# One 512-column matmul for both parts of x in the first feed-forward projections of a two-block transformer

## The chip, the cores and the metric

The kernel runs on one core of one Trainium2 chip. The metric is device time in microseconds (us), the median of the runs shown. The core has a matrix engine (TensorE, PE; its weight loads are PEld), a vector engine (VectorE, DVE), a scalar engine (ScalarE, ACT), GpSimd (POOL) and DMA queues, here issued almost all by SyncE (SP). They run at the same time and wait for each other by semaphores. Matmul results land in PSUM, eight banks of 128 x 512 fp32 values; everything else is in SBUF, 128 partitions wide.

## What is computed

Two transformer blocks of two layers each, on 256 tokens of width 1024, all in fp32. The parts that the change touches are the feed-forwards; the mixers and attentions around them stay as they are.

```python
def squared_relu_mlp(h, w1, w2):      # 1024 -> 4096 -> 1024, once in each layer of the first block
    a = jax.nn.relu(h @ w1)
    return (a * a) @ w2

def swiglu(x, w_in, w_out):           # 1024 -> 2 x 2816 -> 1024, twice in each layer of the second
    gate, up = jnp.split(x @ w_in, 2, axis=-1)
    return (jax.nn.silu(gate) * up) @ w_out

# first block:  x = x + rmsnorm(squared_relu_mlp(rmsnorm(x, g4), w1, w2), g5)
# second block: h = h + 0.5 * swiglu(rms_norm(h, norm), w_in, w_out)
```

## The kernel before, in words

Activations lie transposed: 128 features of a chunk on the partitions, 256 tokens along the row, eight chunks for the width of 1024. To reach fp32 accuracy every matmul operand is a sum of two fp32r values, a high part (rounded) and a low part (the rest), and every product is three matmuls that accumulate into the same place of a bank: high weight x high x (L216), low weight x high x (L217), high weight x low x (L218), all in `mm3`. The x operands are two tiles, `xhi` and `xlo`, or, for the inner activations, pieces of work tiles that the trace calls `u`.

The weights come in 568 groups of 128 x 1024. `load` fetches one by SP's DMA queue into one of six `raw` tiles; `split` makes `rhi` on ScalarE (L203) and `rlo` = raw - rhi on VectorE (L241), in two halves of 512 columns, into a ring of seven. `take` hands a group to a stage, `done` frees it, and `pump` splits ahead as far as the ring reaches. A scheduler places the instructions of a stage on each engine by their dependences, so an engine's order is not that of the source.

A feed-forward of the second block (`ffn`) has 22 jobs. Job j is `W1(j)`: two groups (gate and up), 8 chunks of x each, so 16 products, 48 matmuls, into the two halves of one bank that `bank()` picks in turn from banks 4 to 7. Then `evac_row` multiplies the bank by the norm's factor per token on VectorE (L209, `u<-ps,rst`), ScalarE takes the Silu, VectorE multiplies by the other half, ScalarE and VectorE make the high and low parts. `W2(j - 2)` follows on TensorE: 24 matmuls that accumulate into banks 0 to 3, which hold the eight output chunks. The last two chunks of `W2` are done by `rows_tail`, bank by bank, so that the closing work of a bank (the residual sum on VectorE, L212 `xres<-ps,xres`) can start while the other banks still accumulate. The MLP of the first block (`mlp`) is alike with 16 jobs of two groups; its first two jobs run together, product by product (`W1(0, 1)`), then the sums of squares for the norm are taken by `rstd_row` (matmuls L447 on a bank from `bank()`), and the evacuation is one VectorE instruction with the relu (L212 `u<-ps,rst`).

The SBUF tiles are allocated one after another in `Kern.__init__`; `xhi` and `xlo` are the columns 12 to 2060 of tiles of 2064, so they begin 48 bytes past the tile's start.

Of the kernel before, what the change touches and what calls it, by code (L numbers as in the profile page):

```python
# [9 lines left out]
F32R = mybir.dt.float32r  # L10
# [91 lines left out]

class Kern:
    def __init__(self, nc, tc, ctx, d):
# [12 lines left out]
        self.rhi = [R(1024, f"rhi{i}") for i in range(RING)]  # L117
        self.rlo = [R(1024, f"rlo{i}") for i in range(RING)]
        self.x = F(2048, "xres")
        self.xh, self.xl = (R(2064, nm)[:, 12:2060] for nm in ("xhi", "xlo"))  # L120
        self.ssum = F(512, "ssum")
        self.sqb = [F(512, f"sqb{i}") for i in range(2)]
        self.nrm = [F(8, f"nrm{i}") for i in range(3)]
# [4 lines left out]
        self.inv = F(64, "inv")  # L128
        self.lbc = F(12, "lbc")
        self.mx = [F(16, f"mx{i}") for i in range(4)]  # L130
# [133 lines left out]
    def proj(self, out, spec, xh=None, xl=None):  # L264
        xh = self.xh if xh is None else xh
        xl = self.xl if xl is None else xl
        wh, wl = self.take(spec)
        for k in range(8):
            self.mm3(out, wh[:, k * 128:(k + 1) * 128], wl[:, k * 128:(k + 1) * 128],
                     xh[:, k * 256:(k + 1) * 256], xl[:, k * 256:(k + 1) * 256], k == 0, k == 7)  # L270
        self.done()

    def projs(self, jobs, xh=None, xl=None):

        xh = self.xh if xh is None else xh
        xl = self.xl if xl is None else xl
        ws = [[self.take(spec) for spec in specs] for _, specs in jobs]
        for k in range(8):
            for (ps, _), w in zip(jobs, ws):
                for o, (wh, wl) in enumerate(w):  # L280
                    self.mm3(ps[:, o * 256:(o + 1) * 256], wh[:, k * 128:(k + 1) * 128], wl[:, k * 128:(k + 1) * 128],
                             xh[:, k * 256:(k + 1) * 256], xl[:, k * 256:(k + 1) * 256],
                             k == 0 and o == 0, k == 7 and o == len(w) - 1, skip=True)
        self.done(sum(len(w) for w in ws))

    def proj_toks(self, jobs, name, xh=None, xl=None):
        xh = self.xh if xh is None else xh
        xl = self.xl if xl is None else xl
        ws = [[self.take((name, "tok", c0, h)) for h in range(2)] for _, c0 in jobs]
        R = lambda z: z.bitcast(F32R)  # L290
        for k in range(8):
            for (ps, _), w in zip(jobs, ws):
                wh, wl = (R(z[:, (k % 4) * 256:(k % 4 + 1) * 256]) for z in w[k // 4])
                for t in range(2):
                    ah = R(xh[:, k * 256 + t * 128:k * 256 + (t + 1) * 128])
                    al = R(xl[:, k * 256 + t * 128:k * 256 + (t + 1) * 128])
# [6 lines left out]
    def proj_tok(self, ps, name, c0, xh=None, xl=None):  # L303
        self.proj_toks([(ps, c0)], name, xh, xl)

    def proj_wide(self, pss, name, c0, xh=None, xl=None):

        xh = self.xh if xh is None else xh
        xl = self.xl if xl is None else xl
        R = lambda z: z.bitcast(F32R)  # L310
        for q in range(4):
            wh, wl = self.take((name, "wide", c0, q))
            for k in (2 * q, 2 * q + 1):
                h, l = (R(z[:, (k % 2) * 512:(k % 2 + 1) * 512]) for z in (wh, wl))
                for t in range(2):
                    ah = R(xh[:, k * 256 + t * 128:k * 256 + (t + 1) * 128])
                    al = R(xl[:, k * 256 + t * 128:k * 256 + (t + 1) * 128])
# [34 lines left out]
    def prep(self, c, gain, x=None, xh=None, xl=None):  # L352
        x = self.x if x is None else x
        xh = self.xh if xh is None else xh
        xl = self.xl if xl is None else xl
        g = self.gc(gain[0], gain[1] * 8 + c)
        X, H, L = (self.chunk(t, c) for t in (x, xh, xl))
# [3 lines left out]
    def prep_hi(self, c, gain):  # L361
        g = self.gc(gain[0], gain[1] * 8 + c)
        self.act(self.chunk(self.xh, c).bitcast(F32R), self.chunk(self.x, c), AF.Identity, scale=g)

    def prep_lo(self, c, gain):
        g = self.gc(gain[0], gain[1] * 8 + c)
        self.stt(self.chunk(self.xl, c).bitcast(F32R), self.chunk(self.x, c), g, self.chunk(self.xh, c),
                        ALU.mult, ALU.subtract)
# [73 lines left out]
    def rstd_row(self):  # L442

        ps = self.bank()
# [24 lines left out]
    def start(self):  # L469
# [27 lines left out]
        self.mh, self.ml = self.big(2, F32R), self.big(2, F32R)  # L497
        self.jobs = []

    def mem_start(self, mem):  # L500
        for b in range(4):
            self.a.dma_start(mem[:, b * 512:(b + 1) * 512], self.d["mem"][:, b * 512:(b + 1) * 512])
        for b in range(4):
            for c in (2 * b, 2 * b + 1):
                self.prep(c, ("mg", 0), mem, self.mh, self.ml)
# [938 lines left out]
```

## Time and profile before

| | |
|---|---|
| median of 3 runs | 1817.27 us (1816.97 to 1817.39) |
| the profiled execution | 1817.29 us, its span 1815.6 us |
| busy, share of the span | PE 97%, PEld 95%, DVE 68%, ACT 57%, POOL 6% |
| DMA | 307.80 MB, mean 170 GB/s |
| matmuls | 14362, of them 12720 from L216 to L218 |

A matmul's own duration in the trace (some 0.28 us for 256 columns) covers its way through the array, and consecutive ones overlap; the distance from one start to the next is what the engine's time is made of. Timeline rows give the start and the duration in us, and an "x2" where the view put two alike in one row. The span is measured on the core; the device time of the same execution is 1.7 us more.

### The profile page before, as it was taken

How to read it: one execution, taken by the hardware profiler on the slowest of the kernel's cores; microseconds unless marked ns; L12 is line 12 of the kernel's file. 1: busy time of each engine (PE TensorE's matmuls, PEld its weight loads, DVE VectorE, ACT ScalarE, POOL GpSimd, SP SyncE). 2: the span in 40 equal slices, each digit the busy share in tenths (PEclk: the TensorE clock that was granted, in tenths of full speed). 3: DMA queues.
4: the chain of work that ended last, by engine and by line, in shares of the span. 5: the costliest groups of instructions: out<-in, count | busy, mean ns of one | idle time of the engine just before them, and what ended most of it. 6: DMA issues, size and time to landing. Idle time of an engine off the chain costs nothing.

```text
span 1815.6 us, 35979 instructions
## 1 busy us (share of the span) xinstructions
PE 1768.7 (97%) x14362; PEld 1722.0 (95%) x14362; DVE 1241.9 (68%) x2261; ACT 1033.0 (57%) x2037; POOL 110.3 (6%) x128
## 2 busy tenths in 40 slices
PE   8899999999999989998999999999999999999997
PEld 7899999999889989998999998999999999899997
DVE  7877786557787685557656778766586566876564
ACT  6556565556566465555544667645465455774453
POOL 2420000000000000000000002000010000200000
PEclk9999999999999999999999999999999999999999
DMA  7434446554654435554555553455545555335551
GB/s 278 158 117 140 160 141 211 187 186 157 223 167 136 158 127 189 188 189 143 187 192 190 174 176 133 170 185 182 196 166 188 188 179 177 121 129 187 196 176 35
DMA packets 85624, 307.80 MB, mean 170 GB/s; under 512 B 9680, under 2 KB 10320, under 8 KB 85456
## 3 DMA queue, kind: packets, MB, share of 16 engines
q1 hardware_dynamic: 83952, 300.92, 48.9%
q0 software_dynamic: 640, 3.15, 0.6%
q8 instruction: 112, 1.84, 0.4%
q10 hardware_dynamic: 864, 1.44, 0.2%
q14 instruction: 56, 0.46, 0.1%
HBM read 304.42 MB, written 1.05 MB: 168 GB/s over the span
## 4 chain that ended last, share of the span: by engine, by line
PE 87%; DVE 6%; ACT 3%; issue 2%; POOL 1%; DMA 1%; DVEq 0%; SPq 0%; ACTq 0%
PE ps L218 25%; PE ps L217 25%; PE ps L216 25%; DVE rlo L241 2%; ACT u L191 1%; PE ps L300 1%; PE ps L299 1%; PE ps L318 1%; PE ps L298 1%; PE ps L320 1%; PE ps L319 1%; PE ps L911 1%; DVE u L212 1%; DVE u L209 1%; PE ps L929 1%
## 5 line engine op out<-in xcount | busy, mean ns | idle before, releaser
L203 ACT CAST rhi<-raw 128x512 fp32r<-128x512 f32 (+1 forms) x1138 | 670.4, 618 | 630.3 <-PE ps L218 591.8
L241 DVE TENSOR_TENSOR rlo<-raw,rhi 128x512 fp32r<-128x512 f32 (+1 forms) x1138 | 760.0, 692 | 336.0 <-ACT rhi L203 331.0
L216 PE MATMUL ps<-xhi,rhi 128*128 128x256 f32 x2560 | 721.8, 282 | 16.1 <-ACT xhi L191 9.5
L218 PE MATMUL ps<-xlo,rhi 128*128 128x256 f32 x2560 | 724.1, 283 | 4.8 <-DVE xlo L212 4.8
L217 PE MATMUL ps<-xhi,rlo 128*128 128x256 f32 x2560 | 724.5, 283 | 0.0
L216 PEld LDWEIGHTS ps<-xhi,rhi 128*128 128x128 f32 x2560 | 488.5, 191 | 18.8 <-ACT xhi L191 10.7
L218 PEld LDWEIGHTS ps<-xlo,rhi 128*128 128x128 f32 x2560 | 484.7, 189 | 7.0 <-DVE xlo L212 6.7
L217 PEld LDWEIGHTS ps<-xhi,rlo 128*128 128x128 f32 x2560 | 485.1, 190 | 0.7 <-DVE rlo L241 0.3
L216 PE MATMUL ps<-u,rhi 128*128 128x256 f32 x1680 | 474.3, 282 | 0.0
L217 PE MATMUL ps<-u,rlo 128*128 128x256 f32 x1680 | 471.0, 280 | 0.0
L218 PE MATMUL ps<-u,rhi 128*128 128x256 f32 x1680 | 471.0, 280 | 0.0
L216 PEld LDWEIGHTS ps<-u,rhi 128*128 128x128 f32 x1680 | 317.5, 189 | 0.9 <-issue 0.7
L218 PEld LDWEIGHTS ps<-u,rhi 128*128 128x128 f32 x1680 | 317.3, 189 | 0.7 <-DVE u L206 0.6
L217 PEld LDWEIGHTS ps<-u,rlo 128*128 128x128 f32 x1680 | 317.3, 189 | 0.4 <-issue 0.2
L209 DVE TENSOR_TENSOR u<-ps,rst 128x512 f32<-128x512 f32 (+1 forms) x129 | 84.0, 655 | 105.2 <-PE ps L218 104.8
L209 POOL TENSOR_TENSOR ssum<-ssum,sqb 128x512 f32<-128x512 f32 x26 | 38.0, 1463 | 1268.8 <-ACT sqb L191 1267.2
L191 ACT ACTIVATE u<-u 128x256 f32<-128x256 f32 (+3 forms) x158 | 86.3, 549 | 35.3 <-PE ps L701 17.5
L206 DVE TENSOR_TENSOR u<-u,u 128x256 fp32r<-128x256 f32 (+2 forms) x128 | 66.4, 519 | 10.3 <-ACT u L203 10.1
L203 ACT CAST u<-u 128x256 fp32r<-128x256 f32 (+2 forms) x128 | 61.9, 483 | 11.5 <-POOL u L1176 7.5
L212 DVE SCALAR_TENSOR_TENSOR xlo<-xres,gain,xhi 128x256 fp32r<-128x256 f32 x96 | 56.9, 620 | 3.0 <-ACT xhi L191 3.0
L191 ACT ACTIVATE xhi<-xres,gain 128x256 fp32r<-128x256 f32 x96 | 43.4, 500 | 26.2 <-DVE xres L209 19.7
L209 DVE TENSOR_TENSOR u<-u,u 128x256 f32<-128x256 f32 (+2 forms) x107 | 51.1, 479 | 0.6 <-ACT u L191 0.5
(170 smaller groups left out, 1260.0 us busy)
## 6 DMA issues: line engine op xcount, KB each, us to landing
raw<-w SPq DMA_DIRECT2D x567, 512.0 KB, 3.9
u<-bias POOLq DMA_DIRECT2D x8, 384.0 KB, 3.9
xres<-x SPq DMA_DIRECT2D x4, 256.0 KB, 5.4
u<-mem ACTq DMA_DIRECT2D x4, 256.0 KB, 3.6
raw<-w SPq DMA_DIRECT2D x2, 256.0 KB, 4.4
u<-tabs SPq DMA_DIRECT2D x1, 512.0 KB, 4.2
out<-u SPq DMA_DIRECT2D x2, 256.0 KB, 2.7
u<-masks SPq DMA_DIRECT2D x1, 256.0 KB, 6.9
```

Source lines behind the costliest of these rows:

```text
L191: i = self.a.activation(out, in_, func, scale=scale, **kw)
L203: return self.a.copy(out.bitcast(F32R), in_)
L206: return self.v.tensor_tensor(out.bitcast(F32R), in_, hi, ALU.subtract)
L209: return (eng or self.v).tensor_tensor(out, a, b, op)
L212: return self.v.scalar_tensor_tensor(out, a, s, b, op0, op1)
L216: self.pe.matmul(out, R(wh), R(xh), start=start, stop=False, skip_group_check=skip)
L217: self.pe.matmul(out, R(wl), R(xh), start=False, stop=False, skip_group_check=skip)
L218: self.pe.matmul(out, R(wh), R(xl), start=False, stop=stop, skip_group_check=skip)
L241: b = self.v.tensor_tensor(l[:, c].bitcast(F32R), r[:, c], h[:, c], ALU.subtract)
L298: self.pe.matmul(o, ah, wh, start=k == 0 and t == 0, stop=False, skip_group_check=True)
L299: self.pe.matmul(o, ah, wl, start=False, stop=False, skip_group_check=True)
L300: self.pe.matmul(o, al, wh, start=False, stop=k == 7 and t == 1, skip_group_check=True)
```

## The change

`xhi` and `xlo` become one tile `xpair` in which every chunk's high part (256 columns) is followed by its low part (`Pair`). A new `projs2` is used for the first projections of `mlp` and `ffn` alone. For each product it issues one matmul of 512 columns, high weight x (high, low), over a whole bank, and one of 256 columns, low weight x high x, into the second half. The sum of the two halves of a bank is then the result. So a job of two groups now has two banks (`pair_bank`: 4 and 5, or 6 and 7), and `halves` adds the halves of each by a VectorE reduction into the SBUF tile that the old evacuation now reads and writes. `rstd_row` of these stages uses bank 3. All other products still go through `mm3`, with views of `xpair`. The order of the small tiles is changed so that `xpair` begins at a multiple of 512 bytes and `rlo` 480 bytes past one.

The core of the diff; the other hunks replace the pair of arguments `xh, xl` by `xp` everywhere.

```diff
@@ class Kern, __init__ @@
         self.rhi = [R(1024, f"rhi{i}") for i in range(RING)]
+        self.inv = F(64, "inv")
+        self.mx = [F(16, f"mx{i}") for i in range(3)]
+        self.nrm = [F(8, "nrm0")]
         self.rlo = [R(1024, f"rlo{i}") for i in range(RING)]
+        self.nrm.append(F(8, "nrm1"))
         self.x = F(2048, "xres")
-        self.xh, self.xl = (R(2064, nm)[:, 12:2060] for nm in ("xhi", "xlo"))
+        self.xp = Pair(R(4096, "xpair"))
...
+    def pair_bank(self):
+        self.nbank += 3 - self.nbank % 2
+        i = 4 + self.nbank % 4
+        return self.psum[i - 1], self.psum[i]
+
+    def projs2(self, jobs):
+
+
+        ws = [[self.take(spec) for spec in specs] for _, specs in jobs]
+        R = lambda z: z.bitcast(F32R)
+        for k in range(8):
+            c = slice(k * 128, (k + 1) * 128)
+            for (ps, _), w in zip(jobs, ws):
+                for o, (wh, wl) in enumerate(w):
+                    self.pe.matmul(ps[o], R(wh[:, c]), R(self.xp.both(k)),
+                                   start=k == 0, stop=False, skip_group_check=True)
+                    self.pe.matmul(ps[o][:, 256:512], R(wl[:, c]), R(self.xp.h(k)),
+                                   start=False, stop=k == 7, skip_group_check=True)
+        self.done(sum(len(w) for w in ws))
+
+    def halves(self, out, pair):
+
+        for o, ps in enumerate(pair):
+            self.v.tensor_reduce(self.chunk(out, o), ps.rearrange("p (s b) -> p b s", s=2), AX.X, ALU.add)
...
-    def rstd_row(self):
-
-        ps = self.bank()
+    def rstd_row(self, ps=None):
+
+        ps = self.bank() if ps is None else ps
...
@@ mlp @@
-            pss = [self.bank() for _ in js]
-            self.projs([(p, [("w_ff1", "col", l, (2 * j + o) * 128) for o in range(2)]) for p, j in zip(pss, js)])
+            pss = [self.pair_bank() for _ in js]
+            self.projs2([(p, [("w_ff1", "col", l, (2 * j + o) * 128) for o in range(2)]) for p, j in zip(pss, js)])
             if "r" not in st:
-                st["r"] = self.rstd_row()
+                st["r"] = self.rstd_row(self.psum[3])
             for ps, j in zip(pss, js):
                 t, a, ah, al = B[j % m]
-                self.stt(self.two(t), self.two(ps), 0.0, self.row(st["r"], 2), ALU.max, ALU.mult)
+                self.halves(t, ps)
+                self.stt(self.two(t), self.two(t), 0.0, self.row(st["r"], 2), ALU.max, ALU.mult)
...
@@ ffn @@
-            pss = [self.bank() for _ in js]
+            pss = [self.pair_bank() for _ in js]
             jobs = [(p, [(wi, "col", l, o + j * 128) for o in (0, DFF)]) for p, j in zip(pss, js)]
             for j in jobs:
-                self.projs([j])
+                self.projs2([j])
...
-                self.evac_row(t, ps, st["r"])
+                self.halves(t, ps)
+                self.evac_row(t, t, st["r"])
```

TensorE in the third of the four feed-forwards of the second block, at the end of its last first projection (job 21) and the beginning of a second projection, before. `u116` holds the inner activation of job 19, the number behind an underscore is a tile's running number:

```order
L216 MATMUL ps6_117<-xhi_89,rhi5_79 128x256
L217 MATMUL ps6_117<-xhi_89,rlo5_86 128x256
L218 MATMUL ps6_117<-xlo_90,rhi5_79 128x256
L216 MATMUL ps6_117<-xhi_89,rhi6_80 128x256
L217 MATMUL ps6_117<-xhi_89,rlo6_87 128x256
L218 MATMUL ps6_117<-xlo_90,rhi6_80 128x256
L216 MATMUL ps0_111<-u116_14200,rhi0_74 128x256
L217 MATMUL ps0_111<-u116_14200,rlo0_81 128x256
L218 MATMUL ps0_111<-u116_14200,rhi0_74 128x256
```

The same place in the change; the lines of the file have moved, L251 to L253 are now `mm3`:

```order
L332 MATMUL ps6_116<-xpair_95,rhi5_79 128x512
L334 MATMUL ps6_116<-xpair_95,rlo5_91 128x256
L332 MATMUL ps7_117<-xpair_95,rhi6_80 128x512
L334 MATMUL ps7_117<-xpair_95,rlo6_92 128x256
L251 MATMUL ps0_110<-u116_13135,rhi0_74 128x256
L252 MATMUL ps0_110<-u116_13135,rlo0_86 128x256
L253 MATMUL ps0_110<-u116_13135,rhi0_74 128x256
```

Three matmuls of 256 columns have become one of 512 and one of 256, and the two groups of the job write two banks.

VectorE at the same place: the evacuation of job 21, the product with the gate, the low part (`u115` as output) and the first closing sum, before:

```order
L241 TENSOR_TENSOR rlo6_87<-raw3_71,rhi6_80 128x512
L209 TENSOR_TENSOR u112_14196<-ps6_117,rst2_103 128x512
L241 TENSOR_TENSOR rlo5_86<-raw2_70,rhi5_79 128x512
L209 TENSOR_TENSOR u114_14198<-u114_14198,u112_14196 128x256
L241 TENSOR_TENSOR rlo6_87<-raw3_71,rhi6_80 128x512
L206 TENSOR_TENSOR u115_14199<-u114_14198,u115_14199 128x256
L241 TENSOR_TENSOR rlo0_81<-raw4_72,rhi0_74 128x512 x2
L212 SCALAR_TENSOR_TENSOR xres_88<-ps0_111,xres_88 128x512
```

And in the change, where L341 is `halves`, L276 the split of the weights, L244 the evacuation and the gate product, L241 the low part, L247 the closing sum:

```order
L276 TENSOR_TENSOR rlo6_92<-raw3_71,rhi6_80 128x512
L341 TENSOR_REDUCE u112_13131<-ps6_116 128x256
L341 TENSOR_REDUCE u112_13131<-ps7_117 128x256
L276 TENSOR_TENSOR rlo5_91<-raw2_70,rhi5_79 128x512
L244 TENSOR_TENSOR u112_13131<-u112_13131,rst2_106 128x512
L276 TENSOR_TENSOR rlo6_92<-raw3_71,rhi6_80 128x512
L244 TENSOR_TENSOR u114_13133<-u114_13133,u112_13131 128x256
L276 TENSOR_TENSOR rlo0_86<-raw4_72,rhi0_74 128x512
L241 TENSOR_TENSOR u115_13134<-u114_13133,u115_13134 128x256
L276 TENSOR_TENSOR rlo0_86<-raw4_72,rhi0_74 128x512
L247 SCALAR_TENSOR_TENSOR xres_94<-ps0_110,xres_94 128x512
```

Two reductions and one more split stand between the end of the first projection and the evacuation.

TensorE at the end of the same feed-forward (`rows_tail`; rhi0 and rlo0 are weights of chunk 19, rhi1 of chunk 20, rhi2 of chunk 21), before:

```order
L216 MATMUL ps3_114<-u116_14200,rhi0_74 128x256
L217 MATMUL ps3_114<-u116_14200,rlo0_81 128x256
L218 MATMUL ps3_114<-u116_14200,rhi0_74 128x256
L216 MATMUL ps0_111<-u115_14199,rhi1_75 128x256
L217 MATMUL ps0_111<-u115_14199,rlo1_82 128x256
L218 MATMUL ps0_111<-u115_14199,rhi1_75 128x256
L216 MATMUL ps0_111<-u115_14199,rhi2_76 128x256
L217 MATMUL ps0_111<-u115_14199,rlo2_83 128x256
L218 MATMUL ps0_111<-u115_14199,rhi2_76 128x256
L216 MATMUL ps0_111<-u115_14199,rhi1_75 128x256
L217 MATMUL ps0_111<-u115_14199,rlo1_82 128x256
```

In the change, from the third of the four banks on:

```order
L251 MATMUL ps2_112<-u115_13134,rhi1_75 128x256
L252 MATMUL ps2_112<-u115_13134,rlo1_87 128x256
L253 MATMUL ps2_112<-u115_13134,rhi1_75 128x256
L251 MATMUL ps3_113<-u115_13134,rhi1_75 128x256
L252 MATMUL ps3_113<-u115_13134,rlo1_87 128x256
L253 MATMUL ps3_113<-u115_13134,rhi1_75 128x256
L251 MATMUL ps0_110<-u115_13134,rhi2_76 128x256
L252 MATMUL ps0_110<-u115_13134,rlo2_88 128x256
L251 MATMUL ps1_111<-u115_13134,rhi2_76 128x256
```

Before, the first product of chunk 21 (rhi2) followed one product of chunk 20 (rhi1); now it follows four, one for each of the banks 0 to 3, so nine matmuls of chunk 20 have moved ahead of it.

## Rows read from the trace of the kernel before

**Rows 1.** The profile's page: busy, granted clock, and the chain that ended last.

```profile
span 1815.6 us, 35979 instructions
...
PE 1768.7 (97%) x14362; PEld 1722.0 (95%) x14362; DVE 1241.9 (68%) x2261; ACT 1033.0 (57%) x2037; POOL 110.3 (6%) x128
...
PEclk9999999999999999999999999999999999999999
...
PE 87%; DVE 6%; ACT 3%; issue 2%; POOL 1%; DMA 1%; DVEq 0%; SPq 0%; ACTq 0%
PE ps L218 25%; PE ps L217 25%; PE ps L216 25%; DVE rlo L241 2%; ACT u L191 1%; PE ps L300 1%; PE ps L299 1%; PE ps L318 1%; PE ps L298 1%; PE ps L320 1%; PE ps L319 1%; PE ps L911 1%; DVE u L212 1%; DVE u L209 1%; PE ps L929 1%
```

**Rows 2.** Timeline of TensorE, 1511 to 1520 us (start, duration, engine, line, operation).

```profile
1511.36 0.28 PE L216 MATMUL ps<-u,rhi 128*128 128x256 f32 x1
...
1514.16 0.28 PE L216 MATMUL ps<-xhi,rhi 128*128 128x256 f32 x1
...
1519.83 0.28 PE L216 MATMUL ps<-u,rhi 128*128 128x256 f32 x1
```

**Rows 3.** Timeline of TensorE where it has 512 columns.

```profile
453.05 0.39 PE L318 MATMUL ps<-rhi,xhi 128*128 128x512 f32 x1
...
458.60 0.39 PE L318 MATMUL ps<-rhi,xhi 128*128 128x512 f32 x1
...
1130.12 0.62 PE L1223 MATMUL ps<-u,exact 128*128 128x512 f32 x2
1130.57 0.40 PE L1225 MATMUL ps<-u,exact 128*128 128x256 f32 x2
```

**Rows 4.** Groups of VectorE by form: count | busy, mean ns | idle before.

```profile
L209 DVE TENSOR_TENSOR u<-ps,rst 128x512 f32<-128x512 f32 x113 | 77.5, 690 | 105.0 <-PE ps L218 104.8
...
L403 DVE TENSOR_SCALAR nrmw<-ps 128x256 f32<-128x256 f32 x16 | 6.7, 416 | 2.2 <-ACT nrmw L191 2.2
...
L870 DVE TENSOR_REDUCE mx<-ps 128x2 f32<-128x512 f32 x8 | 5.5, 689 | 3.5 <-PE ps L911 3.5
```

**Rows 5.** Busy us (and instructions) of PE, PEld, DVE, ACT, POOL by stretch; clock.

```profile
240.00:434.00 194.00, 193.91 (x1646) 193.50 (x1645) 126.88 (x208) 108.29 (x191) 2.84 (x2) 1.00 0.54 185
...
1352.00:1534.00 182.00, 182.00 (x1548) 181.84 (x1547) 114.09 (x199) 91.26 (x174) 2.34 (x3) 1.00 0.55 188
```

**Rows 6.** Timelines at the third feed-forward's end: DVE, then PE.

```profile
1528.49 0.69 DVE L209 TENSOR_TENSOR u<-ps,rst 128x512 f32<-128x512 f32 x1 [1.19 <-PE ps L218]
1529.10 0.68 DVE L241 TENSOR_TENSOR rlo<-raw,rhi 128x512 fp32r<-128x512 f32 x1
1529.70 0.42 DVE L209 TENSOR_TENSOR u<-u,u 128x256 f32<-128x256 f32 x1
...
1531.39 0.42 DVE L206 TENSOR_TENSOR u<-u,u 128x256 fp32r<-128x256 f32 x1 [0.67 <-ACT u L203]
...
1528.29 0.28 PE L216 MATMUL ps<-u,rhi 128*128 128x256 f32 x1
...
1531.44 0.35 PE L216 MATMUL ps<-u,rhi 128*128 128x256 f32 x1
```

**Rows 7.** Timelines at the start of the first MLP: PE, then DVE.

```profile
253.83 0.28 PE L216 MATMUL ps<-xhi,rhi 128*128 128x256 f32 x1
...
265.02 0.28 PE L218 MATMUL ps<-xlo,rhi 128*128 128x256 f32 x1
...
265.38 0.47 PE L216 MATMUL ps<-xhi,rhi 128*128 128x256 f32 x1
...
256.52 0.68 DVE L209 TENSOR_TENSOR u<-ps,mrst 128x512 f32<-128x512 f32 x1
...
261.25 0.68 DVE L209 TENSOR_TENSOR u<-ps,mrst 128x512 f32<-128x512 f32 x1
```

**Rows 8.** Waits of TensorE for x: in all, times, longest; then one in its timeline.

```profile
PE ps L218 <- DVE xlo L212: 4.8, 8, 1.6
...
1541.46 0.39 PE L218 MATMUL ps<-xlo,rhi 128*128 128x256 f32 x1 [0.77 <-DVE xlo L212]
```

## What I expected before the run

> **What bounds the kernel now.** I read the busy shares first, then the chain that ended last: TensorE is busy for 97% of the span, and 87% of the chain is TensorE work, of which the three matmul lines of the shared product helper (L216, L217, L218) carry 25% each [rows 1]. VectorE is busy for 68%. The granted TensorE clock is at its upper level, 2.4 GHz, in all 40 slices [rows 1]. So the time is the number of matmuls times the distance from one start to the next, plus the few places where TensorE waits. The "mean ns of one" of a matmul group is no price, because matmuls overlap; I price by start to start. The waits of TensorE on the feed-forward operands are short: 4.8 us in 8 waits of L218 for the low part of x [rows 8].
>
> The distances, from the timeline of TensorE. In the third of the four feed-forwards a first projection runs from 1514.16 to 1519.83, 48 matmuls of 256 columns in 5.67 us: 118.1 ns each, 354.4 ns for the three passes of a product. The 24 matmuls of the second projection before it, of the same shape, take from 1511.36 to 1514.16: 2.80 us, 116.7 ns each [rows 2]. So a matmul of 256 columns costs 116.7 to 118.1 ns, and what differs between the two is only where their operands lie. For 512 columns the kernel has its own example: from 453.05 to 458.60 run 24 of them, 5.55 us, 231.3 ns each; two others, from 1130.12 to 1130.57, take 225 ns each [rows 3].
>
> The Trainium skill, page "TensorE: Matmul & The Clock Gate", section "Back-to-back issue gap", gives the gap of a single matmul at the full clock as its columns over 2.4 plus about 2.5 ns, which makes an estimated 109.2 and 215.8 ns here. The trace does not agree: its distances are 7% longer, so they decide; the rule comes back beside a rival, since by it the fused matmul saves only one fixed 2.5 ns.
>
> **The change part by part.** *Fused matmuls.* The first projections of both MLPs (2 x 32 column groups) and of the four feed-forwards (4 x 44) are 240 groups of 8 products, 1920 products. Each falls from three matmuls of 256 columns to one of 512 and one of 256, so 5760 matmuls become 3840. A pair costs between 225 + 116.7 = 341.7 and 231.3 + 118.1 = 349.4 ns. I take 346 (229 + 117): 229 since the 24 in a row weigh more than the two, less something because the new buffer for x starts at a multiple of 512 bytes and the low weights are put 480 bytes past one, an arrangement nearer to that of the 116.7 ns matmuls than the old one. Saving: 354.4 - 346 = 8.4 ns x 1920 = **16.1 us**; ends 5.0 ns (9.6 us) and 12.7 ns (24.4 us). No row shows a 512-column matmul with these operands, so no saving at all stays an outer end (last rival).
>
> *Other matmuls whose addresses change.* 640 products with x in other stages and 1680 with an activation move, the first perhaps to the better distance, the others perhaps away from it. Between 116.7 and 118.1 the difference is 1.4 ns a matmul; over 1920 matmuls that is 2.7 us one way, over 5040 it is 7 us the other way. I take **0**.
>
> *The sums on VectorE.* Every one of the 120 jobs (pairs of groups) now has two reductions of one bank, 128x512 to 128x256, ahead of its old evacuation, which then reads SBUF. The nearest row is the 689 ns reduction L870 that reads 128x512 from a bank, though to 128x2; the plain evacuations of 128x512 take 690 [rows 4]. I take 0.69 us; bounds 0.42 (an operation over 128x256, the size written, from a bank) and twice 0.69. That is 2 x 0.69 x 120 = 166 us of VectorE work. It costs TensorE nothing where it is covered: in the third feed-forward 22 jobs fill 182 us with 114.1 us of VectorE work [rows 5], 5.2 us in a period of 8.3 us, and become 6.6; in the first MLP 126.9 us over 16 jobs, 7.9 in a period of 12.1, become 9.3. The cover goes if the reduction takes over (8.3 - 5.2) / 2 = 1.5 us.
>
> *End of each feed-forward.* The last job's result is needed at once. Now: evacuation at 1528.49, a split, the gate product at 1529.70, the low part at 1531.39; TensorE ends the first projection at 1528.29, covers with 24 matmuls of the second projection, and reaches the last operand at 1531.44 [rows 6]. In the change two reductions and one split stand ahead of the evacuation: 3 x 0.60 (VectorE's starts in a row, 1528.49 to 1529.10) = 1.8 us later. The new order puts nine more matmuls of the operand before last ahead, 9 x 0.117 = 1.05 us. What is left is a stall of 0.8 us, plus bank 0 finishing later than the stage's closing work wants it; I take **1.0 us x 4 = 4 us** (0 to 2 each).
>
> *Start of each MLP.* The first two jobs run together and now fill all four rotating banks, where two were used. The third job starts 0.36 us after the last matmul of the second, 265.02 to 265.38 [rows 7]. Its banks are free only after two reductions of the first job, which start when TensorE ends: 2 x 0.60 + about 0.15 of handover less 0.36 = **1.0 us x 2 = 2 us** (1 to 3). In the first MLP the evacuations of memory jobs at 256.52 and 261.25 still hold two of the banks when the second job wants to start at 253.8 [rows 7]; the order moves its matmuls behind the first job's 16 pairs (5.5 us), which covers most. I take **1.3 us** (0 to 2.5).
>
> *First matmul of a stage.* It needs the low part of x as well, two matmuls (0.23 us) earlier than now, in six stages: **1.2 us** (0 to 3; the longest such wait now is 1.6 us, the one shown 0.77 [rows 8]). The norm's row sums go to bank 3, which nobody uses then: 0.
>
> Sum of costs 8.5 us (2 to 15). Net -16.1 + 8.5 = -7.6. The profiled execution is 1817.29 us, the median 1817.27, so **1809.7 us, say 1810**. Ends: -24.4 + 3 gives 1796; -9.6 + 15 gives 1823.
>
> **Rivals.** *Reduction slow, slower than before.* The reduction reads its bank with a step of 256 elements between the two values that it adds, and no row of before shows such a read. The Trainium skill, page "Advanced Engine Details and Errata", section "PSUM Cachelines", states that every two consecutive elements should be contiguous for best throughput; that speaks against this read, and no run here shows it yet. What would happen: each 0.1 us more per reduction costs 0.2 us at each of four ends and two starts, 1.2 us in all. From 1.5 us VectorE bounds the 88 feed-forward jobs too. At 1.7 us: 12 us from the ends and starts, and (5.2 + 3.4 - 8.3) x 88 = 26 us: 1810 + 38 = **1848**. It ends above before from about 1.3 us per reduction on (7.3 / 12 x 0.1 = 0.6 above 0.69). For it: the step. Against: the product and the reduction over 512 elements of a bank both take 0.69, whatever is done with them [rows 4]. Chance 0.11.
>
> *Fusing saves only a fixed part.* The cost per column stays and only the fixed part of one matmul goes: 2 x 116.7 - 231.3 = 2.1 ns x 1920 = 4 us, against 8.5 us of costs: **1822**; with 5.0 ns it is 1816. For it: the 24 in a row at 231.3. Against: 225 at the other place. Chance 0.22, spread over 1815 to 1823. By the formula of the Trainium skill, page and section as above, the saving would be an estimated 2.5 ns a product, 4.8 us, and the time 1821.
>
> *Addresses do more.* If the new arrangement brings the pair to 342 ns and the other 6960 matmuls (2320 products) gain 1 ns each, the gain is 24 + 7 us against 8.5: **1795**. For it: 116.7 against 118.1 in rows of one shape. Against: only 1.4 ns is seen. Chance 0.12.
>
> *The change does not do what it says.* If a 512-column matmul of these operands ran as two of 256, the distance would be 233 or more and the gain under 3 us: 1823. The order shows one instruction, and the 512-column rows are under two of 256. Chance 0.03.
>
> **How the numbers follow.** Main case 0.52, centred on 1810, its own range 1801 to 1817. About 0.2%, 3.6 us, is what a measurement of this kernel can tell from no change: faster is below 1813.6, slower above 1820.9. Faster: 0.44 of the main case, all 0.12 of the addresses, 0.04 of the fixed part: 0.60. Same: 0.08, 0.11 and 0.02 of the slow reduction: 0.21. Slower: 0.19, from the slow reduction 0.09, the fixed part 0.07, the last 0.03. A range of **1795 to 1823** leaves out most of the slow reduction and little below: 2 in 10.
>
> **What would show it.** Right: W1 stretches of the feed-forward with 32 matmuls in about 5.53 us, 0.13 us less than 5.67; reductions at about 0.69 us; VectorE busy near 1410 us of the span; waits of TensorE for VectorE of about 1 us at each feed-forward end and after the second MLP job. Wrong: a pair above 352 ns (fusing pays nothing), a reduction above 1.3 us, waits for the reductions in the middle of the feed-forwards, or distances of the other matmuls that move by over 1 ns.

## The result, and the profile after

The change makes the kernel slower: 1833.11 us median of 5 runs (1831.7 to 1835.26) against 1817.39 (1816.97 to 1818.32), a ratio of 1.0084 with a 95% interval of 1.0071 to 1.0098. The forecast was 1810, faster. All medians here and below are of executions that agree; one of f3_bank_by_bank, 6189.27 us, is left out. The profiled execution of the change is 1833.55 us, its span 1831.8, 16.2 us more than before.

The page of the change, first the busy shares and the clock, then the groups of the new operations (count | busy us, mean ns of one | idle before):

```profile
span 1831.8 us, 32363 instructions
...
PE 1775.8 (97%) x12442; PEld 1638.9 (89%) x12442; DVE 1377.1 (75%) x2501; ACT 1040.0 (57%) x2037; POOL 108.7 (6%) x128
...
PEclk9999999999999999999999999999999999999999
...
L332 PE MATMUL ps<-xpair,rhi 128*128 128x512 f32 x1920 | 690.5, 399 | 13.9 <-DVE xpair L247 12.7
L334 PE MATMUL ps<-xpair,rlo 128*128 128x256 f32 x1920 | 542.4, 283 | 0.0
...
L341 DVE TENSOR_REDUCE u<-ps 128x256 f32<-128x512 f32 x240 | 155.2, 686 | 102.4 <-PE ps L334 102.1
```

The change does what it says: TensorE has 1920 matmuls fewer, at nearly the same mean granted clock (0.988 of full speed against 0.991), and still the same 97% of a longer span [rows 1]. The reductions take 686 ns, as taken (0.69). VectorE's busy time rises by 135 us, less than the 166 forecast in part because neighbours in a row overlap (two reductions take 1.29 us below, not twice 0.69). The chain that ended last is followed back through 14% of this span only, so it is not used; the starts of TensorE are.

Timeline of TensorE in the third feed-forward of the change (start, duration, engine, line, operation): the beginning of a second projection, of a first projection, and of the next second projection.

```profile
1500.74 0.28 PE L251 MATMUL ps<-u,rhi 128*128 128x256 f32 x1
...
1503.57 0.40 PE L332 MATMUL ps<-xpair,rhi 128*128 128x512 f32 x1
...
1509.23 0.28 PE L251 MATMUL ps<-u,rhi 128*128 128x256 f32 x1
```

The first projection now has 32 matmuls and takes 5.66 us, where 48 took 5.67 [rows 2]: 353.8 ns for a pair. The second projection, which the change does not touch, takes 2.83 us for its 24 matmuls, where it took 2.80: 117.9 instead of 116.7 ns each.

For all further comparisons I use means of start to start over a whole trace, of matmuls that follow each other directly, with those more than 25 ns above the median (waits) left out, and add up the two or three of a product. Before, a product with x takes 353.8 ns and one with an inner activation 350.4. In the change the pair takes 353.6 (233.1 + 120.5) and the inner product 353.6. So 1920 products gain 0.4 us in all, and 1680 lose 5.4 us.

The rest is waits. TensorE's waits in the change (us in all, times, longest), those that are new or longer than in [rows 8]:

```profile
PE ps L332 <- DVE xpair L247: 12.7, 4, 5.7
...
PE ps L253 <- DVE xpair L247: 4.1, 4, 2.1
PE ps L251 <- ACT u L238: 4.1, 5, 1.8
...
PE ps L332 <- DVE u L244: 1.2, 1, 1.2
...
PE ps L253 <- DVE u L247: 0.8, 1, 0.8
```

The end of the third feed-forward in the change, VectorE and then TensorE:

```profile
1543.02 1.29 DVE L341 TENSOR_REDUCE u<-ps 128x256 f32<-128x512 f32 x2 [0.95 <-PE ps L334]
1544.22 0.68 DVE L276 TENSOR_TENSOR rlo<-raw,rhi 128x512 fp32r<-128x512 f32 x1
1544.82 0.69 DVE L244 TENSOR_TENSOR u<-u,rst 128x512 f32<-128x512 f32 x1
...
1546.03 0.42 DVE L244 TENSOR_TENSOR u<-u,u 128x256 f32<-128x256 f32 x1
...
1547.71 0.42 DVE L241 TENSOR_TENSOR u<-u,u 128x256 fp32r<-128x256 f32 x1 [0.66 <-ACT u L238]
...
1547.30 0.28 PE L253 MATMUL ps<-u,rhi 128*128 128x256 f32 x1
1547.73 0.39 PE L251 MATMUL ps<-u,rhi 128*128 128x256 f32 x1 [0.15 <-ACT u L238]
1547.95 0.28 PE L252 MATMUL ps<-u,rlo 128*128 128x256 f32 x1
```

From the first reduction to the evacuation pass 1.80 us, the three steps that the prediction counted. TensorE's gap before the last operand is 0.43 us where 0.12 is usual.

The start of the first MLP, TensorE's first matmul of a second projection before:

```profile
276.90 0.28 PE L216 MATMUL ps<-u,rhi 128*128 128x256 f32 x1
```

And in the change, from the first matmul of the stage on; behind it, in the form of [rows 5], a stretch with its clock:

```profile
255.84 0.40 PE L332 MATMUL ps<-xpair,rhi 128*128 128x512 f32 x1
...
276.57 0.39 PE L251 MATMUL ps<-u,rhi 128*128 128x256 f32 x1 [1.79 <-ACT u L238]
...
277.27 0.63 PE L332 MATMUL ps<-xpair,rhi 128*128 128x512 f32 x1
...
277.91 0.63 PE L332 MATMUL ps<-xpair,rhi 128*128 128x512 f32 x1
...
284.08 0.28 PE L253 MATMUL ps<-u,rhi 128*128 128x256 f32 x1
```

```profile
277.20:280.60 3.40, 3.40 (x12) 2.91 (x11) 1.85 (x4) 1.15 (x2) 0.00 (x0) 0.50 0.67 213
```

Before, the first four jobs take from 253.83 [rows 7] to 276.90, 23.07 us. In the change they end at 284.08, 28.24 us after the first matmul. The new order puts two matmuls of the second projection (276.57) ahead of the fourth job, and TensorE waits 1.79 us there for the inner activation; the second MLP has the same wait, 1.80 us at 683.34. Shortly after the first of these waits the granted clock is 0.50, the lower level of 1.2 GHz, for 3.4 us: a pair then takes 0.64 us (277.27 to 277.91) instead of 0.35.

### The profile page after: what moved, and what is told of

Same layout as the page of the kernel before. It is cut to its first block, busy times and chain, and to the rows that moved or that the text cites. A ratio compares the mean times of both kernels' runs of the same rounds, so it can differ in the third digit from the quotient of the medians.

```text
span 1831.8 us, 32363 instructions
## 1 busy us (share of the span) xinstructions
PE 1775.8 (97%) x12442; PEld 1638.9 (89%) x12442; DVE 1377.1 (75%) x2501; ACT 1040.0 (57%) x2037; POOL 108.7 (6%) x128
## 5 line engine op out<-in xcount | busy, mean ns | idle before, releaser
L276 DVE TENSOR_TENSOR rlo<-raw,rhi 128x512 fp32r<-128x512 f32 (+1 forms) x1138 | 762.2, 694 | 247.5 <-ACT rhi L238 237.2
L332 PE MATMUL ps<-xpair,rhi 128*128 128x512 f32 x1920 | 690.5, 399 | 13.9 <-DVE xpair L247 12.7
L334 PE MATMUL ps<-xpair,rlo 128*128 128x256 f32 x1920 | 542.4, 283 | 0.0
L251 PE MATMUL ps<-u,rhi 128*128 128x256 f32 x1680 | 475.3, 283 | 4.1 <-ACT u L238 4.1
L253 PE MATMUL ps<-u,rhi 128*128 128x256 f32 x1680 | 472.5, 282 | 0.8 <-DVE u L247 0.8
L332 PEld LDWEIGHTS ps<-xpair,rhi 128*128 128x128 f32 x1920 | 363.5, 190 | 99.9 <-DVE xpair L247 14.9
L334 PEld LDWEIGHTS ps<-xpair,rlo 128*128 128x128 f32 x1920 | 362.8, 189 | 0.8
L251 PEld LDWEIGHTS ps<-u,rhi 128*128 128x128 f32 x1680 | 316.9, 189 | 11.5 <-ACT u L238 5.6
L253 PEld LDWEIGHTS ps<-u,rhi 128*128 128x128 f32 x1680 | 316.2, 188 | 1.2 <-DVE u L247 1.0
L341 DVE TENSOR_REDUCE u<-ps 128x256 f32<-128x512 f32 x240 | 155.2, 686 | 102.4 <-PE ps L334 102.1
L251 PE MATMUL ps<-xpair,rhi 128*128 128x256 f32 x640 | 186.2, 292 | 7.0 <-ACT rhi L238 7.0
L253 PE MATMUL ps<-xpair,rhi 128*128 128x256 f32 x640 | 182.1, 285 | 4.1 <-DVE xpair L247 4.1
L252 PE MATMUL ps<-xpair,rlo 128*128 128x256 f32 x640 | 182.2, 285 | 0.0
L251 PEld LDWEIGHTS ps<-xpair,rhi 128*128 128x128 f32 x640 | 122.8, 192 | 8.4 <-ACT rhi L238 7.0
L253 PEld LDWEIGHTS ps<-xpair,rhi 128*128 128x128 f32 x640 | 122.7, 192 | 5.2 <-DVE xpair L247 5.0
L252 PEld LDWEIGHTS ps<-xpair,rlo 128*128 128x128 f32 x640 | 124.4, 194 | 0.7 <-DVE rlo L276 0.3
L244 POOL TENSOR_TENSOR ssum<-ssum,sqb 128x512 f32<-128x512 f32 x26 | 37.6, 1447 | 1285.7 <-ACT sqb L226 1285.5
L241 DVE TENSOR_TENSOR u<-u,u 128x256 fp32r<-128x256 f32 (+2 forms) x128 | 66.5, 520 | 6.3 <-ACT u L238 6.1
```

Source lines behind the costliest of these rows:

```text
L241: return self.v.tensor_tensor(out.bitcast(F32R), in_, hi, ALU.subtract)
L244: return (eng or self.v).tensor_tensor(out, a, b, op)
L251: self.pe.matmul(out, R(wh), R(xh), start=start, stop=False, skip_group_check=skip)
L252: self.pe.matmul(out, R(wl), R(xh), start=False, stop=False, skip_group_check=skip)
L253: self.pe.matmul(out, R(wh), R(xl), start=False, stop=stop, skip_group_check=skip)
L276: b = self.v.tensor_tensor(l[:, c].bitcast(F32R), r[:, c], h[:, c], ALU.subtract)
```

## The experiments

Three theories were on trial. **Columns**: a matmul's distance is its columns, so one of 512 costs what two of 256 do, and nothing can be saved. **Places**: fusing does save, but where the operands lie in SBUF moves every distance, and the new places eat the saving. **VectorE**: its extra reads and writes slow TensorE down. All times are medians; ratios are to the kernel before, run on the same chip.

| kernel | us | ratio (95%) | product with x in a first projection, ns | inner product, ns |
|---|---|---|---|---|
| before | 1817.39 | 1 | 353.8 | 350.4 |
| the change | 1833.11 | 1.0084 (1.0071 to 1.0098) | 353.6 | 353.6 |
| e1_old_places | 1824.28 | 1.0033 (1.002 to 1.0046) | 350.0 | 351.6 |
| e2_new_places_alone | 1824.99 | 1.0042 (1.0027 to 1.0057) | 353.2 | 356.2 |
| e3_two_of_256 | 1834.2 | 1.0089 (1.0074 to 1.0104) | 353.9 | 353.9 |
| e4_no_sums | 1823.45 | 1.0033 (1.0022 to 1.0043) | 353.6 | 353.7 |
| f1_fused_at_32 | 1813.73 | 0.9981 (0.9971 to 0.9991) | 346.8 | 350.1 |
| f2_before_at_32 | 1811.11 | 0.9963 (0.9948 to 0.9977) | 350.7 | 350.6 |
| f3_bank_by_bank | 1830.70 | 1.007 (1.0053 to 1.0087) | 353.5 | 353.7 |
| g1_before_at_16 | 1810.86 | 0.996 (0.9945 to 0.9975) | 350.7 | 350.2 |
| g2_more_at_16 | 1820.46 | 1.0009 (0.999 to 1.0027) | 352.6 | 352.2 |
| g3_fused_at_64 | 1824.74 | 1.0028 (1.0018 to 1.0037) | 349.1 | 352.9 |
| h1_old_form_at_ends | 1807.71 | 0.9941 (0.9925 to 0.9958) | 346.7 | 350.3 |
| h2_at_32_two_of_256 | 1822.22 | 1.0022 (1.0012 to 1.0031) | 351.1 | 351.1 |

(In the kernels with three matmuls everywhere, the column for x holds all 2560 products with x.)

### Old places, new places, two for one, no sums

The change with the places of before:

```diff
-        self.inv = F(64, "inv")
-        self.mx = [F(16, f"mx{i}") for i in range(3)]
-        self.nrm = [F(8, "nrm0")]
         self.rlo = [R(1024, f"rlo{i}") for i in range(RING)]
...
-        self.xp = Pair(R(4096, "xpair"))
+        self.xp = Pair(R(4128, "xpair")[:, 12:4108])
```

> The change with the operand places of before: the low weights at a multiple of 512 bytes again, the tile for x 48 bytes past one; everything else as in the change. Columns theory (a matmul's distance is its columns, so one of 512 costs what two of 256 do, wherever the operands lie): the pair stays at 350 to 354 ns, the products with an activation fall back from 353.8 to 350.3 ns, 1680 x 3.5 = 6 us, so about 1827 us. Places theory (fusing would save, the new places eat it): the pair falls to 346 to 348 as well, 1920 x 7 = 13 us more, so about 1814. VectorE theory (its extra reads and writes slow TensorE's operand reads): nothing changes, 1833.

1824.28 us, 0.5% under the change: the pair at 350.0 ns (232.4 + 117.6) and the inner product at 351.6. 1920 x 3.6 + 1680 x 2.0 = 10 us; the times differ by 9. (The low part of x is not quite where it was: 112 bytes past a multiple of 512 before, 48 here.) It fits the columns theory best, which had let the pair fall to 350; VectorE's theory, with nothing to change, falls.

The places of the change alone, with the old matmuls:

```diff
-            pss = [self.pair_bank() for _ in js]
-            self.projs2([(p, [("w_ff1", "col", l, (2 * j + o) * 128) for o in range(2)]) for p, j in zip(pss, js)])
+            pss = [self.bank() for _ in js]
+            self.projs([(p, [("w_ff1", "col", l, (2 * j + o) * 128) for o in range(2)]) for p, j in zip(pss, js)])
...
-                self.halves(t, ps)
-                self.evac_row(t, t, st["r"])
+                self.evac_row(t, ps, st["r"])
```

> The places of the change alone: x in one tile of alternating parts, low weights 480 bytes past a multiple of 512, but three matmuls of 256 columns, one bank for a job and no sums, as before. Columns theory: the products with an activation are at 353 to 354 instead of 350.3 ns, first projections about 353, so 1817 + 6 = 1823 us. Places theory: the first projections too become slower by what the fused matmul lost, 7 ns x 1920 = 13 us, so about 1836. VectorE theory: places do nothing, 1817.

1824.99 us. Moving operands costs 7 us without any change to the work: the inner product goes from 350.4 to 356.2 ns (9.7 us), the products with x from 353.8 to 353.2 (1.5 us back). The inner products lie here as they do in the change, where they take 353.6: so place alone does not settle the distance.

The 512-column matmul written as two:

```diff
-                    self.pe.matmul(ps[o], R(wh[:, c]), R(self.xp.both(k)),
-                                   start=k == 0, stop=False, skip_group_check=True)
+                    self.pe.matmul(ps[o][:, 0:256], R(wh[:, c]), R(self.xp.h(k)),
+                                   start=k == 0, stop=False, skip_group_check=True)
+                    self.pe.matmul(ps[o][:, 256:512], R(wh[:, c]), R(self.xp.l(k)),
+                                   start=False, stop=False, skip_group_check=True)
```

> The change with its 512-column matmul written as two of 256 columns (high weight x high x, high weight x low x), same banks, places and sums. Columns theory: 2 x 117.5 for 235, no change in time, 1833 plus or minus 3 us. Forecast's theory (fusing saves 8 ns a product, the loss is elsewhere): 1833 + 16 = 1849. Places theory: as columns theory, within 3 us.

1834.2 us and 353.9 ns for a product, as the change. At these places fusing saves 0.3 ns a product. Up to here the columns theory had the better of it.

The reductions left out:

```diff
-                self.halves(t, ps)
-                self.evac_row(t, t, st["r"])
+                self.evac_row(t, ps[1], st["r"])
```

> The change without the two reductions of a job: the evacuation reads the second bank of the pair as it is, so the sums of the halves and the first bank's results are left out of the computation. VectorE has the work of before. Columns theory: the products stay at 353.8 ns and the pair at 353 to 355; only the waits at the ends and starts go, 8 to 9 us, so about 1825. VectorE theory: pair and products fall to 348 and 350 as well, 10 + 6 us more, so about 1809.

1823.45 us: the sums cost 9 to 10 us, and the distances stay at 353.6 and 353.7 ns. So VectorE's 155 us of reductions do not lengthen the distances; they cost waits, and perhaps clock. Of the waits shown above, those for ACT's `u` and the 0.8 us for VectorE's `u` are gone; the 1.2 us for VectorE's `u` (L244) stay at 1.1, so they are not the sums'. The mean granted clock over the runs is 0.9915 here and 0.989 in the change. An estimate of the most that this can be worth is (0.9915 - 0.989) x 1830 = 4.6 us, so up to half of the 9 to 10 us may have gone by way of the clock.

### Better places, and a scan of them

Since the inner activations lie 32 bytes past a multiple of 512 and their products took 350 ns, x was put there, first in the change; the diff is to e1:

```diff
-        self.xp = Pair(R(4128, "xpair")[:, 12:4108])
+        self.xp = Pair(R(4128, "xpair")[:, 8:4104])
```

> The change with the low weights at a multiple of 512 bytes and x 32 bytes past one, which is where the inner activations lie whose products take 349.9 ns. Places theory: the pair falls from 350.0 ns (x at 48) to 347 or 348, so 1824 - 5 = 1819 us. If 32 has no merit of its own: 350 ns, 1824.

1813.73 us, 19 us under the change with the same instructions. The pair takes 346.8 ns (228.5 + 118.3), within 1 ns of the price that the prediction had taken; the inner product is back at 350.1. Timeline of TensorE in this kernel, the same three starts as above:

```profile
1508.82 0.28 PE L248 MATMUL ps<-u,rhi 128*128 128x256 f32 x1
...
1511.62 0.39 PE L329 MATMUL ps<-xpair,rhi 128*128 128x512 f32 x1
...
1517.17 0.28 PE L248 MATMUL ps<-u,rhi 128*128 128x256 f32 x1
```

5.55 us for the 32 matmuls instead of 5.66, and 2.80 for the second projection instead of 2.83. Then the same in the kernel before:

```diff
-        self.xh, self.xl = (R(2064, nm)[:, 12:2060] for nm in ("xhi", "xlo"))
+        self.xh, self.xl = R(2056, "xhi")[:, 8:2056], R(2072, "xlo")[:, 0:2048]
```

> The kernel before with both parts of x 32 bytes past a multiple of 512 instead of 48 and 112; nothing else. Places theory: the 2560 products with x go from 353.8 to about 350 ns, 9.7 us, so about 1808 us. If 32 has no merit of its own: 1818.

1811.11 us, 7 us under before by moving two tiles: 350.7 instead of 353.8 ns for 2560 products is 7.9 us. So at the same good places the change (f1, ratio 0.9981) is no faster than the three matmuls (f2, 0.9963): the 3.9 ns a product, 7.5 us, do not pay for the sums.

The two groups of a job one after the other:

```diff
-        for k in range(8):
-            c = slice(k * 128, (k + 1) * 128)
-            for (ps, _), w in zip(jobs, ws):
-                for o, (wh, wl) in enumerate(w):
+        for (ps, _), w in zip(jobs, ws):
+            for o, (wh, wl) in enumerate(w):
+                for k in range(8):
+                    c = slice(k * 128, (k + 1) * 128)
```

> The change with a job's two groups one after the other (8 chunks into one bank, then 8 into the other) instead of alternating product by product. If going to another bank after each pair costs TensorE time, the 256-column matmul falls from 120.5 to about 117.5 ns, 1920 x 3 = 6 us; the first bank's sum can also be taken 2.8 us earlier, which takes 0.6 us off each of the six waits at ends and starts: 1834 - 6 - 4 = 1824. If the bank does not matter: 1834 - 4 = 1830. Columns theory says nothing of banks: 1830.

1830.70 us: 120.4 ns for the 256-column matmul, 120.5 in the change. Going to another bank costs nothing. The wait for ACT's `u` falls from 4.1 to 2.6 us, as earlier sums would have it; the rest of the 2.4 us is not located.

TensorE alone, other engines idle, 32 products in either form at each place (`MOFF` are the offsets of x from a multiple of 512 bytes, `LOFF` those of the low weights):

```diff
+        for a in MOFF:
+            for b in LOFF:
+                three(a, b, 2)
+                two(a, b, 2)
```

> TensorE alone, nothing of the transformer computed: jobs of 16 products as three matmuls of 256 columns and as a pair of 512 and 256, one after the other, for ten places of x and four of the low weights, other engines idle. Columns theory: the pair is shorter than the three by at most 4 ns at every place, 1 to 2 ns in the mean, and both move with the places by several ns. Forecast's theory: the pair is shorter by about 8 ns, at least at the places of the change. VectorE theory: with the other engines idle the distances no longer depend on the places.

Its timeline gives four starts in a row: three matmuls with x at 0 and the low weights at 480 (the places of the change), the pair there, three matmuls with x at 16 and the low weights at 0, and the pair there. Then the same with x at 32 and the low weights at 0, three and pair.

```profile
113.55 0.28 PE L1378 MATMUL ps<-x,wh 128*128 128x256 f32 x1
...
124.85 0.39 PE L1389 MATMUL ps<-x,wh 128*128 128x512 f32 x1
...
136.16 0.28 PE L1378 MATMUL ps<-x,wh 128*128 128x256 f32 x1
...
147.04 0.39 PE L1389 MATMUL ps<-x,wh 128*128 128x512 f32 x1
...
225.80 0.28 PE L1378 MATMUL ps<-x,wh 128*128 128x256 f32 x1
...
236.99 0.40 PE L1389 MATMUL ps<-x,wh 128*128 128x512 f32 x1
...
248.10 0.28 PE L1378 MATMUL ps<-x,wh 128*128 128x256 f32 x1
```

Divided by 32: at the places of the change 353.1 for three and 353.4 for the pair, as in the kernel; with x at 32, 349.7 and 347.2, as in f2 and f1. So the distances are TensorE's own, and VectorE's theory is out. The columns theory in its strict form is out too: over 39 places the pair is 4.6 ns shorter in the mean, and the difference runs from -12 to +24 ns. With x at 16 three matmuls took 340.0, the least seen.

That made 16 look like a gain of 35 us:

```diff
+        x2 = R(4128, "xboth")
+        self.xh, self.xl = x2[:, 4:2052], x2[:, 2052:4100]
```

> The kernel before, three matmuls a product, with both parts of x 16 bytes past a multiple of 512 (in one tile, one after the other). In the scan a product took 340.0 ns there, against 355.0 with x at 48. Places theory: 2560 products x (353.8 - 340.0) = 35 us less, 1783 us. If the scan holds only where the other engines are idle: within 5 us of 1811, what x at 32 gave. Columns theory without places: 1818.

1810.86 us and 350.7 ns: a miss. In the kernel the 340 of the scan does not come. With the inner activations at 16 as well:

```diff
+    def ring16(self, n, width):
+        per = 1000 // width
+        u = [self.unit(F32R) for _ in range(-(-n // per))]
+        return [u[i // per][:, 124 + (i % per) * width:124 + (i % per + 1) * width] for i in range(n)]
```

> The same, and the high and low parts of the inner activations of MLPs and feed-forwards 16 bytes past a multiple of 512 as well, instead of 32. Places theory: 1216 second-projection products from 349.9 towards 340 ns, 12 us less than x at 16 alone: 1771. The order of the weights is another there than in the scan (one x chunk against eight weights), so it may give nothing: then 1783.

1820.46 us, a miss too, and its ten runs spread from 1808.17 to 1826.31, where those of before stay within 4 us. The profiled one has 352.6 and 352.2 ns. In the change, x and the low weights at 64:

```diff
-        self.inv = F(64, "inv")
-        self.mx = [F(16, f"mx{i}") for i in range(3)]
-        self.nrm = [F(8, "nrm0")]
+        self.mx = [F(16, "mx0")]
         self.rlo = [R(1024, f"rlo{i}") for i in range(RING)]
```

> The change with x and the low weights both 64 bytes past a multiple of 512. In the scan a pair took 340.3 ns there, against 353.2 at the places of the change. Places theory: 1920 x (353.6 - 340.3) = 25 us less than the change, 1808 us, the other products as in the change. Columns theory without places: 1834. If the forecast's 8 ns were to come on top: not under 1795.

1824.74 us, between: the pair at 349.1, not the 340.3 of the scan.

> TensorE alone again, nothing of the transformer computed: the three matmuls, the pair, and products in the order of the second projections, for 13 other places of x (steps of 4 bytes up to 28, then 40, 80, 112, 144, 272, 496) and low weights at 0 and 64. If 17/16 of the columns at 2.4 GHz is a floor for both forms (768 columns, 340 ns), no place gives less than 340 to either; if fusing has a saving of its own, some place gives a pair clearly under 340. Products in the order of the second projections: about 350 at no place under 340.

The second scan shows that a place alone does not decide. Three starts with x at 16 and low weights at 0: three matmuls, the pair, and products in the order of the second projections.

```profile
251.12 0.28 PE L1378 MATMUL ps<-x,wh 128*128 128x256 f32 x1
...
262.32 0.39 PE L1389 MATMUL ps<-x,wh 128*128 128x512 f32 x1
...
273.41 0.28 PE L1399 MATMUL ps<-x,wh 128*128 128x256 f32 x1
```

350.0 and 346.6 ns: at the same place of x and of both weights the three matmuls took 340.0 in the first scan and 350.0 here. Of the three other places that both scans have, two gave the same again within 1 ns (x at 16 with low weights at 64, x at 112 with low weights at 0). The third did not: with x at 112 and low weights at 64 both forms took 346.7 in the first scan, and 356.5 and 353.3 here. The programs differ in what ran before, but each scan ran once, so whether the work before makes the difference, or one execution differs from the next, is not shown. In both scans hardly any product is under 340.0 or over 367, and many lie at 340, 346.7, 350, 353.3, 356.6 or 360. The mean saving of the pair is 3.8 ns over the 25 places here. No place of either scan has a pair under 340, so a saving below that floor was not seen. Products in the order of the second projections took what the three matmuls took, within 1 ns, at 24 of 25 places, from 340 to 369 ns and not the 350 expected.

### What remained: fusing by itself, and the sums at the ends

On f1, the last job of each feed-forward in the old form, and in `mlp` likewise the first two jobs:

```diff
-            pss = [self.pair_bank() for _ in js]
+            whole = js[0] < NFF - 1
+            pss = [self.pair_bank() if whole else self.pair_bank()[0] for _ in js]
...
-                self.projs2([j])
+                (self.projs2 if whole else self.projs)([j])
...
-                self.halves(t, ps)
-                self.evac_row(t, t, st["r"])
+                if whole:
+                    self.halves(t, ps)
+                    ps = t
+                self.evac_row(t, ps, st["r"])
```

> The change with x at 32 and the low weights at 0 (1813.7 us), but the jobs whose result is awaited at once in the old form, three matmuls into one bank without sums: the first two jobs of each MLP and the last of each feed-forward (128 of the 1920 products). If the cost of the sums lies at the ends and starts, as forecast (4 + 2 + 1.3 us), it goes: 1813.7 - 7 + 128 x 0.0039 = about 1807. If VectorE's extra work costs in the middle of the stages too: 1811 to 1814.

1807.71 us, the fastest kernel of the study, 0.6% under before. Against f1 the ratio falls from 0.9981 to 0.9941, 7.3 us, which is in sum the 4 + 2 + 1.3 us of the forecast. Against f2, the old matmuls at the same places (0.9963), fusing in this form gains 4 us. TensorE's waits there, the first four: the wait for ACT's `u` (L248) that f1 shares with the change (4.2 us) is nowhere in the list.

```profile
PE ps L329 <- DVE xpair L244: 7.8, 5, 5.7
PE ps L248 <- ACT rhi L235: 7.1, 1, 7.1
PE ps L248 <- ACT xpair L223: 4.8, 1, 4.8
PE ps L748 <- POOL u L241: 4.3, 1, 4.3
```

The other question, with the diff of e3 on f1:

> The change with x at 32 and the low weights at 0, its 512-column matmul written as two of 256, sums and banks as in the change. At the places of the change that made no difference. If fusing does save where the places are better (the scan: 349.9 against 347.0 ns; the kernels: 350.7 against 346.8), 1813.7 + 1920 x 0.0035 = 1820.5. If one of 512 is never better than two of 256: 1814.

1822.22 us and 351.1 ns: at these places the fused matmul saves 4.3 ns a product, 8.3 us, against 8.5 in time.

## Why the prediction was wrong

- **The step that failed** is the price of a pair: "I take 346 (229 + 117)", "an arrangement nearer to that of the 116.7 ns matmuls than the old one". It measured 353.6, above even the upper end of 349.4 that the rows were said to give, so the saving of 16.1 us was 0.4. The last rival's outer end, no saving at all, was what came, though for another reason: the instruction is one of 512 columns, but at the new places it takes 233.1 ns and its partner 120.5. Its own sign of being wrong, a pair above 352 ns, came. f1 shows the price of 346 to be right within 1 ns where x is at 32 and the low weights at 0.
- I had read from [rows 2] that places matter, and then guessed which are good from the size of the numbers alone. e2 shows the new ones to be worse for the work around (7 us), and the rows of before held no evidence for 480. That the two distances there differ "only" by places was not shown either, since the order of the products differs too; the second scan bears it out at 24 of 25 places.
- **Other matmuls**, taken at 0 with 7 us as the outer end: 1680 x 3.2 ns = 5.4 us. The bound was right, the value wrong; and the sums for the two ends, 1796 and 1823, leave these 7 us out. (The ends of the cost terms add up to 1 to 16.5 us, where the sum says 2 to 15.)
- **The floor of the saving.** Even at good places fusing saves 3.9 (f2 against f1) to 4.3 ns (h2), not 8.4: the old 354.4 was itself a bad place, and I had put the good place's gain down to the fusion. The rival on the fixed part, 2.1 to 5.0 ns, was nearer; its 1816 to 1822 is where a kernel at equal places would stand (f1 against f2: 0.2% above). The estimate by the formula of the Trainium skill, page "TensorE: Matmul & The Clock Gate", section "Back-to-back issue gap", was 2.5 ns; h2 measures 4.3, the change itself 0.3, so a fixed amount is not what the runs show.
- **The costs were right in sum, in part by luck.** 8.5 us forecast, 9 to 10 measured with e4, of which h1 takes back 7.3 at the ends and starts (against f1, at about the same mean clock, 0.990 and 0.9896). But the terms were not. The end of a feed-forward was put at 1.0 us; in the third one TensorE needs 0.2 us more from the last first projection to the next stage (1543.18 to 1552.07, before 1528.29 to 1536.99). The start of the first MLP was put at 1.0 + 1.3 us; its first four jobs took some 5 us longer. There the third job, which the forecast had waiting, starts almost at once (the new order lets the first job's sums begin before the second job ends). Instead TensorE waits 1.2 us for the memory jobs and 1.8 us for the inner activation that the new order asks for early, and then runs 3.4 us at 1.2 GHz.
- **The clock** was read as at its upper level in all 40 slices and priced at nothing. The digit 9 of that row means 90% or more; the mean granted clock of the profiled execution before was 0.991. What the fall at 277 us hangs on stays open: f1 has the same wait of 1.80 us at 275.34 and no fall behind it.
- **The slow reduction** did not come: 686 ns against 689 for the reduction of a whole bank [rows 4]. The rule of the Trainium skill on contiguous pairs (page "Advanced Engine Details and Errata", section "PSUM Cachelines") is not borne out for this read; that rival is closed.
- The sum as measured: -0.4 + 5.4 + 9.5 = 14.5 of the 15.7 us; the missing microsecond is not located. The earlier need of the low x, put at 1.2 us, was not tried alone.

## What to carry to other kernels

On a kernel that TensorE bounds, moving an SBUF tile is a change to be measured by itself: here the same instructions ran from 1813.7 to 1833.1 us by places alone, more than the whole edit was worth. An edit should then be judged against the old work at the same places: f1 is under the kernel before and not under f2. Before an edit that changes work and places together is costed, the places should be held fixed or each half run alone. Where an edit lengthens a chain, use the old form for the few jobs whose result is awaited at once: that turned 1813.7 into 1807.7.

## What the runs showed of the hardware that was not expected

- The distance of back-to-back matmuls depends on where moving and stationary operands lie, with all other engines idle: 340.0 to 372 ns for the same three matmuls, often on a few levels 3.3 or 6.7 ns apart. What in the chip makes the levels stays open.
- A place does not fix it: 340.0 and 350.0 ns at one place in two scans, 350.7 in the kernel, and 353.6 and 356.2 ns for inner products at one place in two kernels. Whether the work before decides, or something that changes from one execution to the next, was not tried.
- The first scan of TensorE alone foretold the pair in the kernels within 1 ns with x at 0, 32 and 48 (353.4, 347.2 and 349.8 ns against 353.6, 346.8 and 350.0). It missed by 11 ns for the three matmuls with x at 16, and by 9 for the pair with x at 64.
